# An encoder layer on one core: stores moved to ScalarE, v of the fourth kind sorted as it is stored, conditioning and combination spread over more token steps

## Chip, cores and metric

The kernel runs on one NeuronCore of a Trainium2 chip. The metric is the device time of one execution in microseconds (us), lower is better. Profiles show one execution each; the engines are called PE (TensorE, matmul), PEld (its weight loads), DVE (VectorE), ACT (ScalarE), POOL (GpSimd) and SP (SyncE).

## The reference

One layer of an encoder, float32, 1024 tokens of width 1024:

```python
mod = silu(c) @ w_ada + b_ada                      # conditioning: 6 rows of 1024
h = rms_norm(x, g_norm1) * (1 + sc1) + sh1
qa, ka, va, qb, kb, vb, gates = split(h @ w_in)
o_a = neighbourhood_attention(norm(qa), norm(ka), va, rpb)      # 8 heads, 16 x 64 grid
for g, (window, dilation) in enumerate(((128, 1), (512, 4), (2048, 16))):
    outs[g], lses[g] = dilated_window_attention(rot(norm(qb_g)), rot(norm(kb_g)), vb_g, window, dilation)
o_b = einsum(softmax(lses over g), outs)           # the three dilations combined
gate_a, gate_b = split(sigmoid(gates + b_gate))
x = x + gt1 * ((gate_a * (o_a @ w_proj_a) + gate_b * (o_b @ w_proj_b)) @ w_o)
h2 = rms_norm(x, g_norm2) * (1 + sc2) + sh2
a, up = split(h2 @ w_ffn_in)
x = x + gt2 * ((silu(a) * up) @ w_ffn_out)
```

## The kernel before

Every matrix product is made of three passes: each operand is rounded to a short part (whi, by ScalarE, L118) and the remainder (wlo, by POOL or VectorE, L119), and hi·hi, hi·lo and lo·hi are summed in PSUM.

The program has a start (normalisation, first conditioning rows), the **token steps** (about 60 to 615 us of the span), and an end (output projections and the feed-forward part). The change lies in the token steps, the loop `for n in range(6, 92)` with `u, t = divmod(n, 8)`:

- For u below 10, step n projects token tile t (128 tokens) to q, k and v of unit u: 8 chunks of three matmuls 128x384 (L305). A unit is a pair of heads. Kinds 0, 1 and 2 are the three dilations, two units each; **the fourth kind** (kind 3, units 6 to 9) is the neighbourhood attention. For the steps 80 to 91 the chunks are those of the gate product instead (`gate_pre`, L704), whose results are stored by SyncE (sig_d, L711).
- After the chunks, `proj_post` squares and copies q and k (ScalarE), sums (VectorE, L326), takes the reciprocal root (L129 to L134), and, for kinds 1 to 3, copies v to a tile vs (L343) and stores it to v_d in DRAM (L345). At the unit's last tile v is read back with its rows in the order that the kind's attention wants: for kind 3 by eight strided reads (L358).
- Between chunk 4 and chunk 5 stands the attention of earlier units. Before step 58 it works in clusters at odd steps; from step 58 on (`PAIRED`) in items at every step: scores (L468), softmax (L482 to L486), transposes (L494), their evacuation to PT (L498, L500), product with v (L509), evacuation to stg by VectorE (L512) and store by SyncE (L513). Clusters have L588 and L590 for the last two.
- `ada_step` adds one of 64 pieces of the conditioning: w_ada is loaded in pieces of 512 KB (wa, L288), one per two pieces, and VectorE adds it to acc (L292, L294). After eight pieces `ada_row` sums over partitions on PE (L271) and stores a row to mod_d (row, brow).
- `combine_prep` and `combine_step` combine the three dilations, in twelve parts: a part loads ut from DRAM (L643 to L650), VectorE spreads the factors to fb (L655), PE transposes fb (L664), and VectorE multiplies and adds (L672 to L675), at last storing to o_d (L677). Part ci = n − 64 is prepared at step n and taken at step n + 1.

The order on TensorE is that of the code (written out by hand). The orders on the other engines and on the queues come from a scheduler that models a timeline, with priorities (`urgent`), and each tile waits for a free buffer of its tag. One tag matters here: `raw`, six buffers of 128x512, holds the weights on their way to whi and wlo (`wload`), and also the combination's ut and fb and the conditioning's row and brow. The gate weights of step n and n + 1 are two such tiles, taken at even n by `gate_w` at the first chunk.

Of the kernel before, what the change touches and what calls it, by code (L numbers as in the profile page):

```python
# [12 lines left out]
AF = mybir.ActivationFunctionType  # L13
# [23 lines left out]
PAIRED, RBT, COMB = 58, 5, 64  # L37
# [6 lines left out]
def hybrid_layer(ctx: ExitStack, tc: tile.TileContext, x, colp, wada1, wada2, bada2, wqkv, wg, wpa, wpb,  # L44
                 wo, w1, w2, hgain, ropeg, rope, rbias, bmask, g2r, out):
    nc = tc.nc
# [104 lines left out]
    def big(name, shape=None, dtype=F32):  # L151
        return ap_.tile(shape or wide, dtype, tag="big", bufs=NBIG, name=name)
# [113 lines left out]
    ada_state = {"i": 0}  # L266
# [41 lines left out]
    def urgent(off):  # L308
        def deco(f):
            def g(*a):  # L310
                with tc.high_priority(off):
                    return f(*a)
            return g
        return deco

    @urgent(PP)
    def proj_post(U, t):
        pd = U.pd[t]
        qn = ap_.tile([128, 4, 64], F32, tag="qn", bufs=7, name="qn")
        U.qn[t] = qn  # L320
        pq = pd[:, :256].rearrange("p (h d) -> p h d", h=4)
        sq = ap_.tile([128, 256], F32, tag="sq", bufs=1, name="sq")
        nc.scalar.activation(sq, pd[:, :256], AF.Square)
        nc.scalar.activation(qn, pq, AF.Copy)
        ss = ap_.tile([128, 4], F32, tag="ss4", bufs=2, name="ss4")
        nc.vector.tensor_reduce(ss, sq.rearrange("p (h d) -> p h d", h=4), axis=mybir.AxisListType.X, op=ALU.add)  # L326
        r = rstd(ap_, 64, 4, ss, "q")
        nc.vector.tensor_tensor(qn, qn, r[:, :, None].to_broadcast([128, 4, 64]), op=ALU.mult)  # L328
        if U.kind < 3:
            ra = ap_.tile([128, 4, 16], F32, tag="ra", bufs=2, name="ra")  # L330
            rb = ap_.tile([128, 4, 16], F32, tag="rb", bufs=2, name="rb")
            tb = U.tab[:, t]
            v4 = lambda z: z.rearrange("p (a b) c -> p a b c", a=2)
            tv = lambda f, c0, c1: tb[:, f, :, None, c0:c1].to_broadcast([128, 2, 2, c1 - c0])
            nc.gpsimd.tensor_tensor(v4(ra), v4(qn[:, :, 0:16]), tv(0, 0, 16), op=ALU.mult)  # L335
            nc.gpsimd.tensor_tensor(v4(rb[:, :, 0:8]), v4(qn[:, :, 8:16]), tv(1, 0, 8), op=ALU.mult)
            nc.gpsimd.tensor_tensor(v4(rb[:, :, 8:16]), v4(qn[:, :, 0:8]), tv(1, 8, 16), op=ALU.mult)
            nc.gpsimd.tensor_tensor(qn[:, :, 0:16], ra, rb, op=ALU.add)
        if U.kind == 0:
            nc.scalar.activation(U.v[:, t, :], pd[:, 256:384], AF.Copy)  # L340
        else:
            vs = ap_.tile([128, 128], F32, tag="vs", bufs=2, name="vs")
            nc.scalar.activation(vs, pd[:, 256:384], AF.Copy)  # L343
            vd = v_d[U.u - 2]
            nc.sync.dma_start(vd[t * 128:(t + 1) * 128, :], vs)  # L345
            if t == 7:
                U.v = big("v", [128, 8, 128])
            if t == 7 and U.kind == 1:
                vv = vd.rearrange("(h i r) d -> h i r d", h=2, r=4)
                uv = U.v.rearrange("p (r h) d -> p h r d", h=2)  # L350
                for j in range(2):
                    nc.sync.dma_start(uv[:, j], vv[j])
            elif t == 7 and U.kind == 2:
                nc.sync.dma_start(U.v, vd.rearrange("(i u) d -> i u d", u=8))
            elif t == 7:
                vv = vd.rearrange("(r j c) d -> j c r d", r=16, c=8)
                for j in range(8):
                    nc.sync.dma_start(U.v[:, j, :], vv[j])  # L358

    @urgent(QT)  # L360
    def qk_turns(tiles, tag):
# [140 lines left out]
    @urgent(AV)  # L502
    def at_pv(I):
        U, nq, nkb = I.U, I.nq, I.nkb
        po = bank("v")
        for i in range(nkb):
            for h in range(2):
                hs = slice(h * 64, h * 64 + 64)
                nc.tensor.matmul(po[hs, :nq], U.v[:, I.kb0 + i, hs], I.PT[h][:, i, :nq],  # L509
                                 start=(i == 0), stop=(i == nkb - 1))  # L510
        st = ap_.tile([128, 128], F32, tag="stg", bufs=3, name="stg")
        nc.vector.tensor_copy(st[:, :nq], po[:, :nq])  # L512
        nc.sync.dma_start(I.dst, st[:, :nq])  # L513
        if I.last:
            unit_out(U)

# [54 lines left out]
    @urgent(AV)  # L571
    def cl_pv(C):
        po = bank("v")
        n, outs = 0, []
        for I in C.items:
            U, nq = I.U, I.nq
            for i in range(I.nkb):
                for h in range(2):
                    hs, c = slice(h * 64, h * 64 + 64), I.c0 + i * 128
                    nc.tensor.matmul(po[hs, n:n + nq], U.v[:, I.kb0 + i, hs], C.PT[h][:, c:c + nq],  # L580
                                     start=(i == 0), stop=(i == I.nkb - 1))
            if outs and outs[-1][0] is I.o:
                outs[-1][3] = n + nq
            else:
                outs.append([I.o, I.q0, n, n + nq])
            n += nq
        st = ap_.tile([128, 512], F32, tag="stg", bufs=3, name="stg")
        nc.vector.tensor_copy(st[:, :n], po[:, :n])  # L588
        for o, q0, a, b in outs:
            nc.sync.dma_start(o[:, q0:q0 + b - a], st[:, a:b])  # L590
        for I in C.items:
            if I.last:
                unit_out(I.U)
# [65 lines left out]
    def combine_step(i):  # L659
        pr, g, hf = i // 6, (i % 6) // 2, i % 2  # L660
        fb, ut, uv, acc = cb[i]
        pf = bank("t")
        for j in range(4):
            nc.tensor.transpose(pf[:, j * 128:(j + 1) * 128], fb[:, j].rearrange("p h d -> p (h d)"), ident)  # L664
        acc = acc[:, hf * 512:hf * 512 + 512]
        n = 1 if g == 0 else (4 if g == 1 else 8)

        def v(z):
            return z if g == 0 else z.rearrange("p (i r) -> p i r", r=n)

        if g == 0:
            nc.vector.tensor_mul(acc, ut, pf)  # L672
        else:
            nc.vector.tensor_mul(v(pf), uv, v(pf))
            nc.vector.tensor_add(acc, acc, pf)  # L675
        if g == 2 and hf == 1:
            nc.sync.dma_start(o_d[4 + pr], cb[i][3])  # L677
# [92 lines left out]
    U = new_unit(0, w0)  # L770
# [136 lines left out]
    for t in range(6):  # L907
        proj_post(U, t)
# [5 lines left out]
    for n in range(6, 92):  # L914
        u, t = divmod(n, 8)
        if u < 10:
            if t == 0:
                units.append(new_unit(u, [nextw[u, k] for k in range(KT)]))
            U = units[u]
# [16 lines left out]
                    ready.setdefault(8 * u + 2 + slot, []).append(I)  # L936
        if n == 8 * 7 + 5:
            combine_stats()
        ci = n - COMB
        if 0 <= ci < 12:  # L940
            combine_prep(ci)
        if n >= PAIRED:
            done, prev, cur = prev, cur, ready.pop(n, [])
# [46 lines left out]
        chunk()  # L990
        chunk()
        chunk()
        if n >= 8 and (t != 7 or u > 8) and ada_state["i"] < 65:
            ada_step()
        if 2 <= u < 6 and t < 5:
            if t in (2, 4):
# [4 lines left out]
                t_piece(2 * (u - 2) + t // 2, 1)  # L1001
        if n in (85, 88):
            w1_combos((n - 85) // 3, EARLY[(n - 85) // 3])
        if 1 <= ci < 13:
            combine_step(ci - 1)
        while chunks:
            chunk()
        if u < 10:
# [649 lines left out]
```

## Time and profile before

| | us |
|---|---|
| median of 3 runs | 1515.14 (1513.23 to 1521.24) |
| the profiled execution | 1508.57 |
| its span | 1506.8 |
| PE busy | 1486.2 (99%) |
| VectorE busy | 1098.1 (73%) |
| ScalarE busy | 656.3 (44%) |
| POOL busy | 537.1 (36%) |
| HBM traffic | 240 MB, 159 GB/s over the span |

A row of a group reads: line, engine, operation, output <- inputs, shape, count | busy time, mean ns of one | idle time of the engine just before them and what ended it. A row of the timeline reads: start, length, instruction, count, and in brackets the idle time before it and its releaser. SPq is SyncE's queue of DMA issues, ACTq is ScalarE's. PE is pipelined, so that its busy time is not its peak; its waits and its granted clock tell more.

### The profile page before, as it was taken

Reading aid. Unit: us, or ns where it says so; the run is one execution under the profiler, and the core shown is the slowest. Engines: PE = TensorE matmul, PEld = TensorE weight load, DVE = VectorE, ACT = ScalarE, POOL = GpSimd, SP = SyncE. Lnnn points to the kernel's source line nnn. Section 1 sums busy time; section 2 is a strip of 40 time slices with the busy share of each in tenths; the row PEclk is TensorE's granted clock in tenths of the full one; section 3 lists DMA queues with packets and bytes.
Section 4 is the critical chain, followed back from the end, with each engine's and each line's share of the span. In section 5 each row is a group of like instructions: output and inputs, shape, how many; then the busy total and the mean of one; then the engine's idle time right before and its main releaser. Section 6 shows DMA issues by size and latency. Waiting matters only on the chain. (4 is left out here: it accounts for less than half of the span.)

```text
span 1506.8 us, 24296 instructions
## 1 busy us (share of the span) xinstructions
PE 1486.2 (99%) x8156; PEld 1265.3 (84%) x8156; DVE 1098.1 (73%) x2318; ACT 656.3 (44%) x1638; POOL 537.1 (36%) x540
## 2 busy tenths in 40 slices
PE   9999999999999999999999999999999999999998
PEld 7999989998878877888888888888888888887886
DVE  6868777777889845466665597788767777599468
ACT  5655555555545543246432344233223323354442
POOL 0432333311100040002352301677767776104464
PEclk9999999999999999999999999999999999999999
DMA  9625444545145155834553225345433334798342
GB/s 371 226 85 186 141 153 143 192 137 166 59 126 169 62 179 154 318 98 126 168 188 137 92 90 186 119 131 182 155 127 108 109 105 147 268 380 280 98 150 102
DMA packets 154415, 241.66 MB, mean 160 GB/s; under 512 B 26657, under 2 KB 73377, under 8 KB 153521
## 3 DMA queue, kind: packets, MB, share of 16 engines
q1 hardware_dynamic: 153136, 235.90, 47.7%
q10 hardware_dynamic: 1152, 4.19, 0.7%
q8 instruction: 65, 1.06, 0.3%
q14 instruction: 62, 0.50, 0.1%
HBM read 179.89 MB, written 60.15 MB: 159 GB/s over the span
## 5 line engine op out<-in xcount | busy, mean ns | idle before, releaser
L119 POOL TENSOR_TENSOR wlo<-raw,whi 128x512 fp32r<-128x512 f32 (+2 forms) x133 | 172.5, 1310 | 463.4 <-ACT whi L118 435.3
L118 ACT ACTIVATE whi<-raw 128x512 fp32r<-128x512 f32 (+1 forms) x348 | 204.1, 599 | 260.0 <-PE ps_s L1493 35.4
L305 PE MATMUL ps_d<-whi,hT 128*128 128x384 f32 x1152 | 311.0, 341 | 0.0
L119 DVE TENSOR_TENSOR wlo<-raw,whi 128x512 fp32r<-128x512 f32 (+1 forms) x215 | 180.5, 852 | 75.2 <-ACT whi L118 70.8
L305 PEld LDWEIGHTS ps_d<-whi,hT 128*128 128x128 f32 x1152 | 210.3, 189 | 5.3 <-ACT vs L343 3.5
L305 PE MATMUL ps_d<-wlo,hT 128*128 128x384 f32 x576 | 193.6, 336 | 2.4 <-DVE wlo L119 2.0
L305 PEld LDWEIGHTS ps_d<-wlo,hT 128*128 128x128 f32 x576 | 108.9, 189 | 3.2 <-DVE wlo L119 2.3
L118 ACT ACTIVATE whi<-ws 128x512 fp32r<-128x512 f32 x65 | 40.8, 628 | 126.4 <-DVE ws L1340 74.2
L1273 POOL TENSOR_TENSOR e<-e,c 128x512 f32<-128x512 f32 x44 | 68.9, 1566 | 61.3 <-DVE c L1403 37.1
L335 POOL TENSOR_TENSOR ra<-qn,rtab 128x64 f32<-128x64 f32 x48 | 16.7, 348 | 153.4 <-DVE qn L328 138.4
L119 POOL TENSOR_TENSOR wlo<-m,whi 128x512 fp32r<-128x512 f32 x35 | 51.3, 1476 | 54.8 <-ACT whi L118 54.8
L1271 ACT ACTIVATE e<-e 128x512 f32<-128x512 f32 x44 | 27.5, 630 | 88.0 <-DVE e L1406 60.7
L547 ACT ACTIVATE P<-P,st 128x256 f32<-128x256 f32 (+2 forms) x100 | 45.5, 457 | 41.0 <-DVE st L545 41.0
L294 DVE SCALAR_TENSOR_TENSOR acc<-wa,cact,acc 128x512 f32<-128x512 f32 x56 | 43.2, 772 | 24.6 <-DMA wa<-in_wada_dram 24.6
L704 PE MATMUL ps_d<-hT,whi 128*128 128x512 f32 x192 | 60.6, 397 | 0.0
L483 ACT ACTIVATE P<-P,sx 128x384 f32<-128x384 f32 (+1 forms) x64 | 37.0, 580 | 51.4 <-DVE sx L482 51.4
L1323 PE MATMUL ps_v<-h2T,whi 128*128 128x512 f32 x192 | 59.2, 389 | 0.0
L1323 PE MATMUL ps_s<-h2T,whi 128*128 128x512 f32 x192 | 59.1, 389 | 0.0
L1323 PE MATMUL ps_d<-h2T,whi 128*128 128x512 f32 x184 | 56.7, 390 | 0.0
L129 ACT ACTIVATE ry<-ss,eps 128x4 f32<-128x4 f32 (+1 forms) x88 | 26.3, 299 | 69.5 <-DVE ss L326 67.2
L119 DVE TENSOR_TENSOR wlo<-ws,whi 128x512 fp32r<-128x512 f32 x45 | 50.3, 1117 | 8.2 <-ACT whi L118 8.1
L1272 DVE TENSOR_TENSOR e<-e 128x512 f32<-128x512 f32 x44 | 42.5, 974 | 17.3 <-ACT e L1271 17.2
(445 smaller groups left out, 3951.6 us busy)
## 6 DMA issues: line engine op xcount, KB each, us to landing
raw<-in_w_dram SPq DMA_DIRECT2D x139, 256.0 KB
ga_d<-e SPq DMA_DIRECT2D x77, 256.0 KB
raw<-ga_d SPq DMA_DIRECT2D x77, 256.0 KB
wa<-in_wada_dram SPq DMA_DIRECT2D x32, 512.0 KB
raw<-in_wqkv_dram SPq DMA_DIRECT2D x80, 192.0 KB
m<-in_w_dram SPq DMA_DIRECT2D x44, 256.0 KB
raw<-in_wg_dram SPq DMA_DIRECT2D x42, 256.0 KB
xt<-in_x_dram SPq DMA_DIRECT2D x16, 512.0 KB
```

Source lines behind the costliest of these rows:

```text
L118: nc.scalar.activation(hi[:, :n], r, AF.Copy)
L119: (eng or nc.gpsimd).tensor_sub(lo[:, :n], r, fview(hi[:, :n]))
L129: nc.scalar.activation(y, ss, AF.Ln, scale=1.0 / n, bias=eps)
L294: nc.vector.scalar_tensor_tensor(ada_acc[c], wa, cact[:, kk:kk + 1], ada_acc[c], op0=ALU.mult, op1=ALU.add)
L305: nc.tensor.matmul(pd[:, :384], tok(a, k, t), U.w[k][b][:, :384], start=(k == 0 and i == 0), stop=(k == KT - 1 and i == 2))
L483: nc.scalar.activation(P[:nq, :nk], P[:nq, :nk], AF.Exp, scale=-1.0, bias=nm, accum_out=sm)
L547: nc.scalar.activation(C.P[h][:nq, c], C.P[h][:nq, c], AF.Exp, scale=-1.0, bias=nm, accum_out=sm)
L704: nc.tensor.matmul(st["p"], gw[i, br][j][a][:, kk * 128:(kk + 1) * 128], hT[b][:, k, hs], start=(k == 0 and q == 0), stop=(k == 7 and q == 2))
L1271: nc.scalar.activation(sg, a, AF.Sigmoid)
L1272: nc.vector.tensor_mul(sg, sg, a)
L1273: nc.gpsimd.tensor_mul(sg, sg, up)
L1323: nc.tensor.matmul(pb, w[p][:, k * 128:(k + 1) * 128], b[q][:, k], start=(k == 0 and i == 0), stop=(k == 3 and i == 2))
```

## The change

1. The 64 stores of v (kinds 1 to 3) and the attention results' stores are issued by ScalarE instead of SyncE; the attention results are evacuated from PSUM by ScalarE instead of VectorE.
2. For kind 3 the store of v scatters the rows to the order that the attention wants, so that one plain read brings it back instead of eight strided ones.
3. From step 58 on, `ada_step` runs at even steps, and at every step after 76 (before: at nearly every step, until step 80; now until step 87).
4. The combination's part ci is prepared at step 64 + 2·ci and taken one step later (before: every step): it ends at step 87 instead of 76.

```diff
-            nc.sync.dma_start(vd[t * 128:(t + 1) * 128, :], vs)
+            if U.kind == 3:
+                nc.scalar.dma_start(vd.rearrange("(c r j) d -> r j c d", c=8, r=16)[2 * t:2 * t + 2], vs)
+            else:
+                nc.scalar.dma_start(vd[t * 128:(t + 1) * 128, :], vs)
...
-                vv = vd.rearrange("(r j c) d -> j c r d", r=16, c=8)
-                for j in range(8):
-                    nc.sync.dma_start(U.v[:, j, :], vv[j])
+                nc.sync.dma_start(U.v, vd.rearrange("(p j) d -> p j d", j=8))
...
-        nc.vector.tensor_copy(st[:, :nq], po[:, :nq])
-        nc.sync.dma_start(I.dst, st[:, :nq])
+        nc.scalar.activation(st[:, :nq], po[:, :nq], AF.Copy)
+        nc.scalar.dma_start(I.dst, st[:, :nq])
...
-        nc.vector.tensor_copy(st[:, :n], po[:, :n])
+        nc.scalar.activation(st[:, :n], po[:, :n], AF.Copy)
         for o, q0, a, b in outs:
-            nc.sync.dma_start(o[:, q0:q0 + b - a], st[:, a:b])
+            nc.scalar.dma_start(o[:, q0:q0 + b - a], st[:, a:b])
...
-        ci = n - COMB
-        if 0 <= ci < 12:
+        ci, odd = divmod(n - COMB, 2)
+        if 0 <= ci < 12 and not odd:
             combine_prep(ci)
...
-        if n >= 8 and (t != 7 or u > 8) and ada_state["i"] < 65:
+        if n >= 8 and (n % 2 == 0 or n > 76 if n >= PAIRED else t != 7) and ada_state["i"] < 65:
             ada_step()
...
-        if 1 <= ci < 13:
-            combine_step(ci - 1)
+        if 0 <= ci < 12 and odd:
+            combine_step(ci)
```

The lines after the change stand up to two higher by number (L345 becomes L346 and L348, L358 becomes L359, L513 becomes L514, L664 becomes L665, L704 becomes L705).

The order on TensorE changes only where the conditioning's sums and the combination's transposes go. Before, at the passage from step 79 (the last chunks of the projection) to step 80 (the gate product):

```order
L305 MATMUL ps_d<-whi,hT_406 128x384
L305 MATMUL ps_d<-whi,hT_112 128x384
L305 MATMUL ps_d<-wlo,hT_112 128x384
L305 MATMUL ps_d<-whi,hT_406 128x384
L704 MATMUL ps_d<-hT_112,whi 128x512
L704 MATMUL ps_d<-hT_406,whi 128x512
L704 MATMUL ps_d<-hT_112,wlo 128x512
```

Now a conditioning sum (acc to ps_t) and the transposes of fb, which end step 79, stand directly ahead of the first gate matmul:

```order
L305 MATMUL ps_d<-whi,hT_112 128x384
L305 MATMUL ps_d<-wlo,hT_112 128x384
L305 MATMUL ps_d<-whi,hT_406 128x384
L271 MATMUL ps_t<-acc_6327,ones 1x512
L665 MATMUL ps_t<-ident,fb 128x128 x4
L705 MATMUL ps_d<-hT_112,whi 128x512
L705 MATMUL ps_d<-hT_406,whi 128x512
L705 MATMUL ps_d<-hT_112,wlo 128x512
```

What moved are those two rows, which stood in earlier steps before; the gate matmuls themselves are the same.

On SyncE, the loads of the gate weights (raw<-in_wg) of step 80 stood before the change among the stores of the projection's v (v_d) and the attention's results (o_d), several steps ahead, with a conditioning weight (wa) before them:

```order
L288 DMA wa_7665<-in_wada_dram 128x1024
L111 DMA raw<-in_wg_dram 128x512
L345 DMA v_d<-vs 128x128
L111 DMA raw<-in_wg_dram 128x512
L274 DMA brow<-in_bada_dram 1x512
L513 DMA o_d<-stg 128x128
L345 DMA v_d<-vs 128x128
L513 DMA o_d<-stg 128x128
L345 DMA v_d<-vs 128x128
L677 DMA o_d<-oacc 128x1024
L513 DMA o_d<-stg 128x128
```

Now the first of them stands behind the combination's load for step 80 (ut), and the second behind the row of the conditioning (mod_d) and the read-back of v:

```order
L288 DMA wa_7669<-in_wada_dram 128x1024
L647 DMA ut<-u_d 128x4x128
L111 DMA raw<-in_wg_dram 128x512
L276 DMA mod_d<-row 1x512
L359 DMA v<-v_d 128x1024
L111 DMA raw<-in_wg_dram 128x512
L647 DMA ut<-u_d 128x4x128
L111 DMA raw<-in_wg_dram 128x512 x2
L651 DMA ut<-u_d 128x8x64
```

What moved: the two loads stand behind transfers of step 79 and 80 instead of some steps ahead of the last stores of v, and v is read once. In the order after the change, the first load's buffer is the one that held fb of the transposes quoted above, and it waits for them.

For the gate weights of step 88, SyncE before had them far ahead, between the stores of the gate results (sig_d) of steps 80 and 81:

```order
L711 DMA sig_d<-gsig 128x512
L111 DMA raw<-in_wg_dram 128x512
L276 DMA mod_d<-row 1x512
L111 DMA raw<-in_wg_dram 128x512 x5
L513 DMA o_d<-stg 128x128
L111 DMA raw<-in_wg_dram 128x512 x4
L711 DMA sig_d<-gsig 128x512
L111 DMA raw<-in_wg_dram 128x512 x3
```

Now they follow the stores of step 86's and step 87's gate results, ahead of the conditioning's last row:

```order
L712 DMA sig_d<-gsig 128x512
L765 DMA w_d<-w1m 128x512 x2
L712 DMA sig_d<-gsig 128x512 x2
L111 DMA raw<-in_wg_dram 128x512
L276 DMA mod_d<-row 1x512
L111 DMA raw<-in_wg_dram 128x512 x2
L678 DMA o_d<-oacc 128x1024
L111 DMA raw<-in_wg_dram 128x512 x12
```

What moved: the first load of step 88 has gone behind both stores of step 87's time, as its buffer is taken after row and brow of the conditioning's last sum, which step 87 makes; w1m and w_d are combinations of the feed-forward part's weights and stand ahead of it.

## The prediction

> **What bounds the kernel now.** I read the page's table of engines first, then the table by stage, then PE's waits, then what stood in front of each. The page's row gives busy time, share of the span and instructions:
>
> ```profile
> PE 1486.2 (99%) x8156; PEld 1265.3 (84%) x8156; DVE 1098.1 (73%) x2318; ACT 656.3 (44%) x1638; POOL 537.1 (36%) x540
> ```
>
> TensorE is the bound, and the change leaves its instructions and nearly their order as they are. So the change can win only what TensorE waits, and only in the stretch that it touches, the token steps (about 60 to 615 us). Stages of that stretch (length, then busy time of PE, PEld, DVE, ACT, POOL, then the granted clock, the DMA share and GB/s):
>
> ```profile
> 364.00:400.00 36.00, 33.74 (x214) 29.24 (x215) 26.58 (x95) 18.05 (x61) 0.40 (x1) 0.95 0.31 108
> 400.00:440.00 40.00, 36.35 (x272) 31.70 (x270) 34.52 (x112) 19.50 (x67) 5.04 (x5) 1.00 0.47 145
> 480.00:530.00 50.00, 47.80 (x347) 41.57 (x346) 43.75 (x144) 24.19 (x82) 2.99 (x2) 1.00 0.30 97
> 530.00:580.00 50.00, 50.00 (x295) 38.55 (x295) 25.39 (x74) 22.97 (x58) 18.49 (x14) 1.00 0.65 197
> ```
>
> VectorE is the fuller of the helpers where the conditioning, the combination and the fourth kind's attention meet (34.5 of 40 us), ScalarE has room (19.5), and the gate steps from 530 us on have no gap at all. PE's waits over 60 to 615 us (total, times, longest):
>
> ```profile
> PE ps_t L494 <- DVE oacc L672: 2.3, 1, 2.3
> PE ps_t L494 <- DVE P L486: 2.1, 2, 1.2
> PE ps_d L305 <- DVE wlo L119: 2.0, 1, 2.0
> PE ps_t L664 <- ACT PT L500: 1.4, 2, 1.1
> PE ps_t L494 <- DVE oacc L675: 1.2, 1, 1.2
> PE ps_v L369 <- POOL qn L338: 0.5, 1, 0.5
> PE ps_v L369 <- DVE qn L328: 0.5, 2, 0.3
> PE ps_d L305 <- POOL wlo L119: 0.4, 1, 0.4
> PE ps_t L494 <- DVE rv L130: 0.4, 1, 0.4
> PE ps_t L664 <- DVE PT L498: 0.3, 1, 0.3
> ```
>
> They add up to 11.1 us. The largest, on TensorE's and then on VectorE's timeline (start, length, instruction, idle time before it and its releaser):
>
> ```profile
> 371.97 0.44 PE L494 MATMUL ps_t<-ident,P 128*128 128x128 f32 x2 [1.24 <-DVE P L486]
> 373.23 0.46 PE L494 MATMUL ps_t<-ident,P 128*128 128x128 f32 x2 [0.82 <-DVE P L486]
> ...
> 425.88 0.44 PE L494 MATMUL ps_t<-ident,P 128*128 128x128 f32 x2 [2.33 <-DVE oacc L672]
> ...
> 429.48 0.66 PE L664 MATMUL ps_t<-ident,fb 128*128 128x128 f32 x4 [1.05 <-ACT PT L500]
> ```
>
> ```profile
> 423.69 1.54 DVE L294 SCALAR_TENSOR_TENSOR acc<-wa,cact,acc 128x512 f32<-128x512 f32 x2 [3.98 <-DMA wa<-in_wada_dram]
> 425.14 0.68 DVE L672 TENSOR_TENSOR oacc<-ut,ps_t 128x512 f32<-128x512 f32 x1
> ```
>
> VectorE stood 3.98 us at a conditioning weight (L294) that had not landed; L672, queued behind it, frees the PSUM bank that L494 needs. The weight was late because of SyncE's queue:
>
> ```profile
> 412.69 4.90 SPq L358 DMA_DIRECT2D v<-v_d  x8
> 417.70 0.40 SPq L345 DMA_DIRECT2D v_d<-vs  x1
> 418.20 0.38 SPq L513 DMA_DIRECT2D o_d<-stg  x1
> 418.62 0.42 SPq L288 DMA_DIRECT2D wa<-in_wada_dram  x1
> ```
>
> Eight issues of the read-back of v take 4.90 us, two stores follow, and only then goes the load; it is used 5.1 us after its issue (423.69 − 418.62).
>
> The pair at 371.97 and 373.23 also cost clock: the row 364:400 has a granted clock of 0.95, so 36 × 0.05 = 1.8 us. The lone 2.33 us at 425.88 left its row at 1.00. All that can be won is therefore 11.1 + 1.8 = 12.9 us, 0.85% of the time.
>
> **The change part by part.**
>
> *Stores to ScalarE, evacuations from VectorE to ScalarE, one read of v instead of eight, conditioning and combination at every other step.* The groups of 364 to 530 us (busy, mean ns; idle before) and ScalarE's own issue of a DMA:
>
> ```profile
> L294 DVE SCALAR_TENSOR_TENSOR acc<-wa,cact,acc 128x512 f32<-128x512 f32 x20 | 15.6, 781 | 8.6 <-DMA wa<-in_wada_dram 8.6
> L674 DVE TENSOR_TENSOR ps_t<-ut,ps_t 128x512 f32<-128x512 f32 x8 | 8.5, 1064 | 0.7 <-PE ps_t L664 0.7
> L129 ACT ACTIVATE ry<-ss,eps 128x4 f32<-128x4 f32 x22 | 6.5, 297 | 28.9 <-DVE ss L326 28.7
> L512 DVE COPY stg<-ps_v 128x128 f32<-128x128 f32 x21 | 6.0, 284 | 0.0
> L818 ACTq DMA_DIRECT2D h_d<-yT x8: 326/326/337, 28.7 to 53.8; - x8
> ```
>
> VectorE loses one 0.28 us copy per step here, half of L294 and half of the combination; SyncE loses 7 × 0.6 = 4.3 us of issues per unit of the fourth kind and both stores of each step. So the conditioning loads go out earlier and are asked for later. I count the L672 wait as gone (2.3), the two L486 waits as gone with their clock (2.1 + 1.8), L675 as 0.4 left (0.8 won), L664 and L119 as halved (0.9 and 1.0), the rest as staying but for 0.3: 9.2 us won. From below: if only the read-back matters, 4; from above, all 12.9.
>
> ScalarE pays per step two issues of 0.33 us and a copy that took VectorE 0.28 us, about 1 us of a step of some 6. The store of v stands ahead of L129, which waits anyway: 28.7 us over 22 steps, 1.3 us per step, for VectorE's sum (L326). So two thirds of it are hidden. If that cover is gone, L129 and all behind it come up to 0.7 us later in a step, and 30 such steps would give at most some 20 us, but only if TensorE waited on each, and L129's results are used two steps on. A store on ScalarE can also stand at its queue for an earlier transfer, with the exponential L483 and the evacuation L500 behind it; before, such waits stood on SyncE and no row shows them on ScalarE. Bounds 0 (the waits are past by then) to 4 us (four waits of the 1.05 us of row 429.48, which is PE waiting for ScalarE); I take 1, one such wait. Nothing below zero, as a store earlier on ScalarE frees nothing that TensorE waits for beyond what is counted.
>
> *The gate weights of step 80.* Here the change adds a wait. The weights' buffers are shared with the combination's tiles (ut, fb) and the conditioning's (row, brow). Before, the combination was over at step 76, and the loads for step 80 went out long ahead (SyncE, then TensorE's first use):
>
> ```profile
> 489.34 0.43 SPq L111 DMA_DIRECT2D raw<-in_wg_dram  x1
> ...
> 491.12 0.33 SPq L111 DMA_DIRECT2D raw<-in_wg_dram  x1
> ```
>
> ```profile
> 524.62 0.63 PE L704 MATMUL ps_d<-hT,whi 128*128 128x512 f32 x2
> ```
>
> 35 us of lead. Now all six buffers are held at step 79 by the combination of steps 76 and 78 and by row/brow, and the first gate load waits for the combination's transposes at the end of step 79, the very instruction in front of the first gate matmul. TensorE then stands for the load, the rounding on ScalarE, and the remainder on POOL. Their prices: load to use on SyncE and ScalarE, and POOL's group.
>
> ```profile
> 534.03 0.38 SPq L111 DMA_DIRECT2D raw<-in_wg_dram  x1
> ...
> 546.20 2.84 SPq L111 DMA_DIRECT2D raw<-in_wg_dram  x3
> ```
>
> ```profile
> 539.06 1.25 ACT L118 ACTIVATE whi<-raw 128x512 fp32r<-128x512 f32 x2 [5.47 <-DMA raw<-in_wg_dram]
> ...
> 544.71 0.68 ACT L710 ACTIVATE gsig<-ps_d,cp 128x512 f32<-128x512 f32 x1
> ...
> 549.18 0.63 ACT L118 ACTIVATE whi<-raw 128x512 fp32r<-128x512 f32 x1 [1.60 <-DMA raw<-in_wg_dram]
> ```
>
> ```profile
> L119 POOL TENSOR_TENSOR wlo<-raw,whi 128x512 fp32r<-128x512 f32 x14 | 18.5, 1345 | 58.9 <-ACT whi L118 58.8
> ```
>
> From issue to first use: 539.06 − 534.03 = 5.0 us with other loads beside it, and 549.18 − 546.20 = 3.0 for the first of three. I take the middle, 4.0, as neither fits better. Then 0.63 of L118, then 1.35 of POOL less the 0.5 us in which TensorE does the two matmuls that need only whi: 4.0 + 0.63 + 0.85 = 5.5 us (4.5 to 6.5).
>
> *The gate weights of step 88.* Same buffers, another queue: the load now stands on SyncE behind the store of step 87's gate result (sig_d), which needs L710 after TensorE's last matmul of step 87. So 0.1 + 0.68 (L710) + 0.36 (a store's issue) = 1.1 us later, less what TensorE still has to do, four transposes (0.66, row 429.48) and one conditioning sum:
>
> ```profile
> L271 PE MATMUL ps_t<-acc,ones 128*1 128x512 f32 x2 | 1.0, 590 | 0.0
> ```
>
> 1.1 + 5.5 − 0.66 − 0.59 = 5.3 us (4.3 to 6.3). The gate steps had no wait to hide it in (50.00 of 50.00). Steps 82, 84, 86 and 90 keep a lead of two steps or more: nothing.
>
> *The clock after those two gaps.* Waits of 2.1 us in all, close together, cost 1.8 us in the row 364:400; a single 2.33 cost none. Gaps of 5.4 are nearer to the first: 1.8 each, 3.6 (0 to 3.6). The Trainium skill, "TensorE: Matmul & The Clock Gate", Part 1: The HAM clock gate, says that the array goes to half clock after a free-running window of about 3.4 us spent idle and needs such a window of work to come back. By it 1.7 us per drop, and a 5.4 us gap holds a whole window in some 6 cases of 10, an estimate of 2.0 us for both instead of 3.6, so a sum lower by 1.6. This trace does not agree with the idle window as told: waits of 1.24 and 0.82 us were enough.
>
> **Sum.** −9.2 + 1.0 + 5.5 + 5.3 + 3.6 = +6.2 us. On the profiled execution's 1508.57 us (span 1506.8) that is 1514.8; that execution lies 6.6 us under the median of the runs, 1515.14, and on the median it is 1521.3, so 1521.
>
> **The rivals.**
>
> *The two stalls and the old waits together (slower).* If the conditioning loads are late because the transfers themselves are slow, and not because of SyncE's queue, VectorE still stands in front of the combination's evacuations. For it: 5.1 us from issue to use at 418.62, with the queue's part over by then. Against it: half of the asks. Then L672, L486 and their clock (6.2 us) stay: +12.4, 1527.5. It decides if more than 1.3 us of those 6.2 remain, as 0.5% is 7.5 us. The Trainium skill, "DMA: Bandwidth & Descriptors", Issuing engines are not separate DMA queues, speaks for it: spreading issues over engines saves only the issuing, since all share the same DMA engines. The issue alone was 4.90 us here, which the trace shows to be no small thing.
>
> *The stalls do not come (faster).* If the loads land in under 3 us and the gate matmuls find their weights with a wait of 1 us or less, the sum is −9.2 + 1 + 2 = −6.2, and −10 with everything won: 1505 to 1509. For it: no such wait stands in the trace of before. Against it: no row of a gate load is shorter than 3.0 us.
>
> *ScalarE becomes what TensorE waits for (slower).* In the combination's steps ScalarE goes from 19.5 of 40 us to about 27, and its stores may stand before L483. 4 us instead of 1 gives +9.2, 1524. Against it: its present waits are mostly on VectorE, which gets lighter.
>
> *It doesn't do what it says.* With the loads no earlier in time and the gaps half as long, gains (4) and losses (6) cancel: +2, 1517.
>
> **How the numbers follow.** My forecast (+2 to +10, 1517 to 1525) has 0.50, of which 0.13 lies beyond 0.5%; late transfers 0.22; ScalarE 0.05; no stalls 0.13, of which 0.08 beyond 0.5%; cancelling 0.10. 0.5%, 7.5 us, is about what a measurement of this kernel can tell from no change. So slower 0.13 + 0.22 + 0.05 = 0.40, faster 0.08, same 0.52. Range: low end −9.2 of gain (the middle) with both stalls at their least and no clock loss, −9.2 + 4.5 + 4.3 = −0.4, widened to −5 for part of the rival without stalls, 1510; high end gain 4, stalls 6.5 + 6.3, clock 3.6, ScalarE 4 = +16.4, 1531.
>
> **What would show it.** Right: in the table by stage, PE loses about 5 us once around 525 us and once around 590 us, with the first gate matmul waiting on whi or wlo and the granted clock below 1 there; L672 and L486 gone from PE's waits; L294's idle time on the load below 8.6 us. Wrong in its main step: gate matmuls that start without a wait, or a gate load issued well ahead of step 79's end. Wrong in the gain: L494 still waiting for L672 or L486.

## The result, and the profile after

The change made the kernel slower: 1524.34 us (median of 6 runs, 1521.78 to 1526.16) against 1516.0 (6 runs, 1511.02 to 1521.24), ratio 1.0064 with a 95% interval of 1.0046 to 1.0081. The forecast was 1521 in a range of 1510 to 1531; the time lies in the range and on the side of the forecast's sum. By the prediction's own line of 0.5% it is "slower", to which 0.40 was given, and not "same", which had 0.52.

The profiled execution has a span of 1522.9 us. Its row of engines, and the stages of the token steps with those of them cut where the gate steps 80 and 88 begin (length, busy time of PE, PEld, DVE, ACT, POOL, then the granted clock, DMA share, GB/s):

```profile
PE 1491.8 (98%) x8156; PEld 1269.1 (83%) x8156; DVE 1083.5 (71%) x2265; ACT 669.7 (44%) x1691; POOL 535.7 (35%) x540
```

```profile
364.00:400.00 36.00, 33.37 (x220) 30.27 (x219) 26.76 (x93) 18.34 (x66) 0.00 (x0) 0.95 0.24 83
400.00:440.00 40.00, 40.00 (x293) 35.01 (x292) 32.79 (x117) 23.95 (x84) 5.30 (x5) 1.00 0.42 130
520.00:540.00 20.00, 16.44 (x93) 12.53 (x94) 7.71 (x31) 7.67 (x21) 5.12 (x4) 0.83 0.48 135
...
580.00:615.00 35.00, 29.88 (x165) 22.23 (x164) 14.73 (x35) 14.39 (x33) 9.98 (x8) 0.90 0.56 171
```

Before, the steps from 530 us on had no gap (50.00 of 50.00); now 20 us around 530 lose 3.6, 35 us before 615 lose 5.1. The stage of the wait for L672 (400 to 440) is full now, and the one before it (364 to 400) is as it was, its clock of 0.95 too. PE's waits (60 to 640 us; the rows of before's table to compare are L672 and the two for L486):

```profile
PE ps_d L705 <- ACT whi L118: 9.9, 2, 5.0
PE ps_s L469 <- DVE qk L395: 2.6, 1, 2.6
PE ps_t L495 <- DVE P L487: 2.2, 1, 2.2
PE ps_d L305 <- DVE wlo L119: 2.0, 1, 2.0
PE ps_v L370 <- POOL qn L338: 1.3, 2, 1.0
PE ps_t L495 <- DVE oacc L676: 0.9, 2, 0.5
PE ps_d L305 <- ACT vs L343: 0.6, 1, 0.6
PE ps_d L305 <- POOL wlo L119: 0.4, 1, 0.4
```

They add up to 19.9 us, 8.8 more than before. The two of 5.0 us are the first gate matmuls of steps 80 and 88. In place, with the load's issue on SyncE and its rounding on ScalarE:

```profile
368.96 0.51 PE L469 MATMUL ps_s<-qk 64*128 64x256 f32 x4 [2.63 <-DVE qk L395]
...
523.43 1.22 PE L705 MATMUL ps_d<-hT,whi 128*128 128x512 f32 x2 [4.96 <-ACT whi L118]
...
595.56 1.22 PE L705 MATMUL ps_d<-hT,whi 128*128 128x512 f32 x2 [4.98 <-ACT whi L118]
...
619.33 0.44 PE L495 MATMUL ps_t<-ident,P 128*128 128x128 f32 x2 [2.18 <-DVE P L487]
```

```profile
518.50 0.33 SPq L111 DMA_DIRECT2D raw<-in_wg_dram  x1
...
582.00 8.11 SPq L712 DMA_DIRECT2D sig_d<-gsig  x2
590.20 0.38 SPq L111 DMA_DIRECT2D raw<-in_wg_dram  x1
...
592.89 15.51 SPq L111 DMA_DIRECT2D raw<-in_wg_dram  x12
608.44 0.91 SPq L759 DMA_DIRECT2D w1m<-in_w_dram  x2
```

```profile
522.75 0.63 ACT L118 ACTIVATE whi<-raw 128x512 fp32r<-128x512 f32 x1 [3.81 <-DMA raw<-in_wg_dram]
...
594.88 1.27 ACT L118 ACTIVATE whi<-raw 128x512 fp32r<-128x512 f32 x2 [5.11 <-DMA raw<-in_wg_dram]
```

The load of step 80 goes out at 518.50, as step 79's transposes end, and that of step 88 at 590.20, behind the stores of sig_d: 4.25 and 4.68 us to first use, as the prediction priced them (3.0 to 5.0).

The third wait, at 619.33, is a follow-up that was not foreseen. The late load of step 88 holds up the twelve loads behind it, so the loads for the feed-forward part's combinations (w1m) go out at 608.44; in the profile before they went out at 592.75. VectorE takes its instructions in order and stands at them, with the softmax's L487 behind:

```profile
366.25 1.54 DVE L294 SCALAR_TENSOR_TENSOR acc<-wa,cact,acc 128x512 f32<-128x512 f32 x2 [4.06 <-DMA wa<-in_wada_dram]
...
368.30 0.61 DVE L395 TENSOR_TENSOR qk<-ps_v,qk 128x256 fp32r<-128x256 f32 x1
...
617.59 0.69 DVE L760 TENSOR_TENSOR w1m<-w1m 128x512 f32<-128x512 f32 x1 [2.94 <-DMA w1m<-in_w_dram]
```

The upper rows are the same figure at 366 us: the conditioning's weight is late there as before (4.06 us), and only the instruction behind it is another one, L395 in place of L486. But it is no longer SyncE's queue that makes it late. Its load and its use in the kernel before, where the load stands behind eight reads of v, and then its load now, behind one read:

```profile
363.70 0.41 SPq L288 DMA_DIRECT2D wa<-in_wada_dram  x1
...
367.73 0.75 DVE L294 SCALAR_TENSOR_TENSOR acc<-wa,cact,acc 128x512 f32<-128x512 f32 x1 [4.07 <-DMA wa<-in_wada_dram]
```

```profile
359.30 0.89 SPq L288 DMA_DIRECT2D wa<-in_wada_dram  x2
```

The load goes out 4.4 us earlier, but the weight is used only 1.5 us earlier: from issue to use it was 4.0 us before and is 6.9 now, and in those 6.9 us the DMA engines are 0.90 busy. The time that the queue gave back went into the transfer.

Behind each of the waits at 523, 595 and 619 us the clock is at half, or a little above, for some 4 us. Behind step 80's wait in the change:

```profile
523.40:525.40 2.00, 1.84 (x4) 1.02 (x5) 0.00 (x0) 0.63 (x1) 1.27 (x1) 0.50 0.72 236
525.40:527.40 2.00, 2.00 (x6) 1.61 (x5) 0.00 (x0) 0.00 (x0) 1.28 (x1) 0.50 0.44 129
527.40:529.40 2.00, 2.00 (x13) 1.20 (x14) 0.00 (x0) 0.63 (x1) 0.72 (x1) 0.95 0.47 133
```

4.0 us at 0.50 is 2.0 us lost. The same reading behind step 88 gives 1.9 (2 us at 0.50 and 2 at 0.55) and behind 619 us 1.7 (2 at 0.64, 2 at 0.51).

So the two profiles add up. From 60 to 640 us: waits +8.8, clock +2.0 +1.9 +1.7, and a wait of 0.9 on a load (L724) at 651 us: +15.3 (the last is not shown to be the change's, as the same load costs 0.7 in the second profile of before), where the spans differ by 1522.9 − 1506.8 = 16.1. That is twice what the medians differ by (8.3). The first profile of before was one of its shorter executions; why, the second one shows, below.

### The profile page after: what moved, and what is told of

Same layout as the page of the kernel before. It is cut to its first block, busy times and chain, and to the rows that moved or that the text cites. A ratio compares the mean times of both kernels' runs of the same rounds, so it can differ in the third digit from the quotient of the medians.

```text
span 1522.9 us, 24174 instructions
## 1 busy us (share of the span) xinstructions
PE 1491.8 (98%) x8156; PEld 1269.1 (83%) x8156; DVE 1083.5 (71%) x2265; ACT 669.7 (44%) x1691; POOL 535.7 (35%) x540
## 4 chain that ended last, share of the span: by engine, by line
PE 78%; DMA 9%; DVE 7%; ACT 3%; issue 2%; POOL 1%; SPq 1%; ACTq 0%; DVEq 0%; POOLq 0%
PE ps_d L305 13%; PE ps_v L1324 7%; PE ps_d L1324 7%; PE ps_s L1324 7%; PE ps_t L1324 6%; PE ps_d L705 4%; PE ps_s L1494 3%; PE ps_d L1494 3%; PE ps_d L1259 2%; PE ps_s L1259 2%; PE ps_v L1494 2%; PE ps_t L1494 2%; DVE wlo L119 2%; DMA wa<-in_wada_dram 2%; PE ps_v L1259 1%
## 5 line engine op out<-in xcount | busy, mean ns | idle before, releaser
L705 PE MATMUL ps_d<-hT,whi 128*128 128x512 f32 x192 | 64.8, 420 | 9.9 <-ACT whi L118 9.9
L294 DVE SCALAR_TENSOR_TENSOR acc<-wa,cact,acc 128x512 f32<-128x512 f32 x56 | 42.1, 751 | 24.6 <-DMA wa<-in_wada_dram 24.4
L483 DVE CUSTOM_DVE_ANT_0 P<-ps_s,rb 128x384 f32<-128x384 f32 (+1 forms) x64 | 31.9, 520 | 29.1 <-PE ps_s L469 29.0
```

Source lines behind the costliest of these rows:

```text
L294: nc.vector.scalar_tensor_tensor(ada_acc[c], wa, cact[:, kk:kk + 1], ada_acc[c], op0=ALU.mult, op1=ALU.add)
L483: nc.vector.tensor_tensor_reduce(P[:nq, :nk], pS[:nq, :nk], I.masks[h], -1.0, 3.0e38, ALU.add, ALU.min, nm)
L705: nc.tensor.matmul(st["p"], gw[i, br][j][a][:, kk * 128:(kk + 1) * 128], hT[b][:, k, hs], start=(k == 0 and q == 0), stop=(k == 7 and q == 2))
```

## The experiments

Each kernel was run beside the kernel before; the ratios are to that, with 95% intervals. An edit is to the changed kernel where no other one is named. Line numbers are those of the kernel at hand.

### Without the third and fourth part

```diff
-        ci, odd = divmod(n - COMB, 2)
-        if 0 <= ci < 12 and not odd:
+        ci = n - COMB
+        if 0 <= ci < 12:
...
-        if n >= 8 and (n % 2 == 0 or n > 76 if n >= PAIRED else t != 7) and ada_state["i"] < 65:
+        if n >= 8 and (t != 7 or u > 8) and ada_state["i"] < 65:
...
-        if 0 <= ci < 12 and odd:
-            combine_step(ci)
+        if 1 <= ci < 13:
+            combine_step(ci - 1)
```

> The change without its third and fourth part (conditioning and combination at the steps of before; stores and evacuations on ScalarE, v of the fourth kind sorted in the store). Theory (the loss is all from the spread, which makes the gate weights of steps 80 and 88 late; the rest gains): no wait at the first gate matmuls, about 8 us under before, 1508. Rival (ScalarE's stores cost): at or over before, 1516 to 1520, with PE waiting for ScalarE. Rival (the gain of 10 us up to step 79 came from the spread): within 3 us of before.

1509.19 us, 0.9972 (0.9955 to 0.9988). No wait at the gate matmuls. So the loss comes from the spread, and the stores with the sorted v are a gain, of half the size that was expected. What is left in PE's waits of it, at the top:

```profile
PE ps_t L665 <- DVE PT L499: 4.3, 2, 2.4
```

The combination still waits, for an evacuation on VectorE (L499) in place of its own. In front of it VectorE stands 2.2 us for a conditioning weight (L294, 418 us), as in the kernel before.

### Only the third and fourth part

The edit is the reverse of the one above, in the kernel before.

> The kernel before with only the third and fourth part (conditioning and combination spread; stores on SyncE as before). Theory: two waits of about 5 us at steps 80 and 88 with the clock lost behind them and the third one at step 91, 20 us in all, less 2 to 5 us for a lighter VectorE: 1531 to 1534. Rival (the spread is harmless, ScalarE's stores cost): within 3 us of before, 1513 to 1519, and no long wait at the first gate matmuls.

1520.88 us, 1.0045 (1.0029 to 1.0061): slower, through the same waits, but by less than expected.

```profile
PE ps_d L704 <- ACT whi L118: 8.3, 2, 4.2
...
PE ps_t L494 <- DVE P L486: 1.4, 2, 0.8
```

The third wait is not there, and L672 has gone: the spread alone, without any store moved, takes the wait for L672 away.

### The gate weights' buffers taken early

```diff
+        if n in (77, 85):
+            gate_w((n - 77) // 4, 0)
         ci, odd = divmod(n - COMB, 2)
```

> The whole change, but the gate weights of steps 80 and 88 take their buffers at steps 77 and 85, ahead of the combination's and the conditioning's tiles. Theory (shared buffers make those loads late): both waits gone, the one at step 91 too, 17 to 21 us under the change, 1503 to 1508, the fastest of all. Rival (the loads are late for another reason, SyncE's queue or the transposes themselves): waits of 5 us stay, 1520 to 1526. Rival (ScalarE's stores cost): waits gone but no faster than before, 1514 to 1518.

1505.88 us, 0.9950 (0.9929 to 0.9970), the lowest median of all: 18 us under the change by two lines that add no work. Both gate waits are gone, and the one at step 91 with them. What is left at the top of PE's waits, beside the 2.2 us at 213 us that every profile so far has in much the same length:

```profile
PE ps_s L469 <- DVE qk L395: 2.4, 1, 2.4
PE ps_t L724 <- DMA tg<-t_d: 1.1, 1, 1.1
```

### The kernel before, once more

> The kernel before once more, unchanged, for a second profile of it. If the waits of the first profile are the same each time, PE waits about 11 us in the token steps with the same two at 372 and 426 us, and the span is 1507. If the medians of before (1516) hold waits that the first profile (1508.57) did not have, they show here as longer or other waits, with a span of 1510 to 1519.

A span of 1513.7 us. PE's waits are nearly those of the first profile (12.3 us in the token steps against 11.1):

```profile
PE ps_t L494 <- DVE oacc L672: 2.8, 1, 2.8
PE ps_t L494 <- DVE P L486: 2.0, 2, 1.2
PE ps_d L305 <- DVE wlo L119: 2.0, 1, 2.0
```

What differs is the clock behind them. The wait of 2.02 us at 213 us stands in both profiles at the same length. The 2 us from 215 on, in the first profile of before and in this one:

```profile
215.00:217.00 2.00, 2.00 (x20) 1.74 (x18) 1.71 (x9) 1.29 (x6) 0.49 (x3) 1.00 0.35 105
```

```profile
215.00:217.00 2.00, 2.00 (x9) 1.56 (x7) 1.67 (x10) 1.05 (x5) 0.74 (x3) 0.50 0.14 40
...
364.00:400.00 36.00, 32.50 (x206) 28.83 (x205) 24.31 (x90) 16.26 (x58) 0.00 (x0) 0.91 0.33 112
400.00:440.00 40.00, 36.97 (x256) 31.95 (x256) 33.40 (x107) 19.71 (x65) 5.45 (x5) 0.96 0.45 139
```

At the same wait the clock stayed at 1.00 in one execution and went to 0.50 in the other; at 425 us the first lost none and this one 40 × 0.04 = 1.6. With 36 × 0.09 = 3.2 and 25 × 0.07 = 1.7 at 213 (0.93 from 205 to 230 us) that makes 6.5 us of clock against 1.8, and with 1.2 more of waits 5.9 of the 6.9 by which the spans differ. So a wait of 2 us costs 2 us or 3.7, and its length does not decide which: of the 13 profiles of this document that have this wait (1.85 to 2.20 us), five lost clock behind it (0.93 from 205 to 230 us) and eight did not (1.00), and each outcome stands beside a wait of 2.02 and beside one of 2.20 us. One profile of a kernel with many such waits is not its median.

### The conditioning spread, the combination as before

```diff
-        ci, odd = divmod(n - COMB, 2)
-        if 0 <= ci < 12 and not odd:
+        ci = n - COMB
+        if 0 <= ci < 12:
...
-        if 0 <= ci < 12 and odd:
-            combine_step(ci)
+        if 1 <= ci < 13:
+            combine_step(ci - 1)
```

> The whole change but for its fourth part: the combination at every step from 64 to 76 as before, the conditioning spread. Theory (it is the combination's ut and fb that hold the gate weights' buffers): no wait at the first gate matmuls of steps 80 and 88. The gain up to step 79 lies between that of no spread (5 us) and of all of it (8 us), so 1506 to 1510 where before is 1514. Rival (the conditioning's late last row, at step 87, is enough to make the load of step 88 late): one wait of 4 to 5 us there, 1514 to 1518.

1521.35 us, 1.0053 (1.0036 to 1.0071): the theory fell. The rival held on the wait at step 88, but not on the time, which is 3 us above its range. With the combination over at step 76, the load of step 88 is as late as ever (PE, then SyncE):

```profile
592.94 1.22 PE L705 MATMUL ps_d<-hT,whi 128*128 128x512 f32 x2 [4.65 <-ACT whi L118]
```

```profile
588.09 0.32 SPq L712 DMA_DIRECT2D sig_d<-gsig  x1
588.50 0.38 SPq L111 DMA_DIRECT2D raw<-in_wg_dram  x1
```

So for step 88 it is the conditioning's last row, which step 87 now makes, and not the combination. It is also not a lack of buffers: the six loads before it were rounded, and their remainders made, by 537 us. The load goes out as VectorE begins the row (L275, 588.39). It waited for its turn behind the row; how the scheduler's order comes to that with buffers empty, no run here shows.

At step 80 the waits are smaller here, 1.63 us for whi and 0.72 for wlo, and of another kind. Both loads went out 20 us ahead, and ScalarE's rounding, which waits for no load, stands behind the last work of step 79 (SyncE, then ScalarE):

```profile
502.80 2.73 SPq L111 DMA_DIRECT2D raw<-in_wg_dram  x2
```

```profile
522.41 1.14 ACT L118 ACTIVATE whi<-raw 128x512 fp32r<-128x512 f32 x2
```

So the conditioning alone does not make the load of step 80 late.

### The spread and the early buffers alone

The edits of the second and the third experiment, in the kernel before: stores on SyncE, evacuations on VectorE, eight reads of v.

> The kernel before with the spread (third and fourth part) and the gate weights' buffers taken early, but with all stores on SyncE, the evacuations on VectorE and eight reads of v. Theory now (the gain up to step 79 comes from the spread, by asking VectorE for less at a time, and not from the stores): 5 to 9 us under before, 1505 to 1509 where before is 1514, and within 3 us of the whole change with early buffers. Rival (the prediction's cause: SyncE's queue relieved of stores and of seven reads brings the loads in time): within 3 us of before, with L672 or L486 still in PE's waits.

1508.24 us, 0.9959 (0.9944 to 0.9975). The theory holds, at the lower edge of its gain: freed of the late loads, the spread is a gain by itself. L672 is gone from PE's waits; L486 is still there with 1.2 us in two waits, as the rival had it.

### Conditioning weights loaded one step earlier

```diff
         if kk % 2 == 0:
-            ada_acc["w"] = big("wa2", [128, 2, 512])
-            nc.sync.dma_start(ada_acc["w"], wada2[c, :, kk:kk + 2, :])
+            ada_acc["w"] = ada_acc.pop(("n", i)) if i else ada_load(i)
...
+        if kk % 2 == 1 and i < 63:
+            ada_acc["n", i + 1] = ada_load(i + 1)
```

(in the kernel with early buffers; `ada_load` holds the two lines removed)

> The whole change with early gate buffers, and each conditioning weight loaded one step of the conditioning earlier. Theory (VectorE stands in order at a late weight, and PE's waits of 2.2 us at 213 and 2.4 us at 369 are behind it): both gone, 3 to 6 us under the whole change with early buffers, 1500 to 1503 where before is 1514. Rival (the loads go out no earlier, as buffers and SyncE's order decide): 1504 to 1507.

1510.82 us, 0.9981 (0.9967 to 0.9995): higher than without it (0.9950, the intervals just overlap), and not the gain of either forecast. Of the two waits one went (at 213 us, 0.4 left) and one stayed (2.6 for qk), and others came, in steps that had none (2.1 more for vs, L350):

```profile
PE ps_s L476 <- DVE qk L402: 2.6, 1, 2.6
PE ps_v L377 <- POOL qn L345: 2.5, 2, 1.7
```

Neither theory had that. Whether the earlier loads took the place of others was not followed up here.

### Only the sorted store of v

```diff
-            nc.sync.dma_start(vd[t * 128:(t + 1) * 128, :], vs)
+            if U.kind == 3:
+                nc.sync.dma_start(vd.rearrange("(c r j) d -> r j c d", c=8, r=16)[2 * t:2 * t + 2], vs)
+            else:
+                nc.sync.dma_start(vd[t * 128:(t + 1) * 128, :], vs)
...
-                vv = vd.rearrange("(r j c) d -> j c r d", r=16, c=8)
-                for j in range(8):
-                    nc.sync.dma_start(U.v[:, j, :], vv[j])
+                nc.sync.dma_start(U.v, vd.rearrange("(p j) d -> p j d", j=8))
```

(in the kernel before)

> The kernel before with only the second part: v of the fourth kind sorted as it is stored (by SyncE) and read back by one transfer. Theory now (the queue's part is the smaller one): 0 to 3 us under before, 1511 to 1514 where before is 1514, with the wait of VectorE at the conditioning weight shorter than 3.98 us but L672 or L486 still in PE's waits. Rival (the prediction's floor: the read-back alone brings 4 us): 1508 to 1510. Third way (a scattered store costs): above before.

1509.42 us, 0.9974 (0.9959 to 0.9989), about 4 us: more than I then thought, and what the prediction gave as its floor for the read-back. The two waits for L486 at 372 us are gone, and with them the clock's loss:

```profile
350.00:400.00 50.00, 48.84 (x335) 43.44 (x333) 41.27 (x138) 27.30 (x89) 5.26 (x5) 1.00 0.36 119
```

L672 is gone too, but not its cause. VectorE still stands at the conditioning weight, 2.59 us in place of 3.98 (the load follows the one read of v and takes 5.5 us from issue to use, 5.1 before), and TensorE waits longer than before, for an evacuation on ScalarE that waits in its turn for VectorE, and loses 1.6 us of clock behind it (0.96 over 400 to 440 us). VectorE's row, then TensorE's:

```profile
415.35 0.75 DVE L294 SCALAR_TENSOR_TENSOR acc<-wa,cact,acc 128x512 f32<-128x512 f32 x1 [2.59 <-DMA wa<-in_wada_dram]
```

```profile
419.38 1.11 PE L665 MATMUL ps_t<-ident,fb 128*128 128x128 f32 x4 [3.36 <-ACT PT L501]
```

The gain is also that of the run without the spread (0.9972), which has the whole first part, stores and evacuations on ScalarE, beside it. So of the first part these two runs show nothing, neither gain nor loss.

### The combination spread, the conditioning as before

```diff
-        if n >= 8 and (n % 2 == 0 or n > 76 if n >= PAIRED else t != 7) and ada_state["i"] < 65:
+        if n >= 8 and (t != 7 or u > 8) and ada_state["i"] < 65:
```

> The whole change but for its third part: the conditioning at the steps of before (its last row at step 80), the combination spread to step 87. Theory now (the conditioning's last rows at steps 79 and 87 take their place among the buffers just ahead of the gate weights, which have to follow them; the combination's tiles alone do no harm): no long wait at the first gate matmuls of steps 80 and 88, 5 to 9 us under before, 1504 to 1508 where before is 1512.5. Rival (the prediction's cause for step 80, the combination's ut and fb hold the buffers): the wait of 5 us at step 80 stays, 1511 to 1516.

1514.96 us, 1.0015 (0.9999 to 1.0032). On the gate weights the theory holds: no wait at the first gate matmuls of steps 80 and 88, though the combination runs to step 87: the loads of step 80 go out at 502.37 and 504.24, 13 us ahead. On the time it missed by 7 us; the time lies in the rival's range, but for another reason. Late waits take their place, VectorE's rows first and PE's behind them:

```profile
566.97 0.69 DVE L760 TENSOR_TENSOR w1m<-w1m 128x512 f32<-128x512 f32 x1 [3.57 <-DMA w1m<-in_w_dram]
...
572.71 0.69 DVE L676 TENSOR_TENSOR oacc<-oacc,ps_t 128x512 f32<-128x512 f32 x1
```

```profile
573.54 0.52 PE L495 MATMUL ps_t<-ident,P 128*128 128x128 f32 x3 [2.81 <-DVE oacc L676]
```

It is the picture of 425 us in the kernel before: VectorE stands at a late load, then works without a gap, the combination's L676 stands in that row, and L495 lacks the bank. The combination was moved into steps in which another late load, w1m, takes the place of wa.

### The second to fourth part with early buffers

The sorted store above, in the kernel with the spread and the early buffers alone; the stores stay on SyncE, the evacuations on VectorE.

> The second, third and fourth part with early gate buffers, the first part left out: stores on SyncE, evacuations on VectorE. Theory (the sorted store and the spread are the gains, ScalarE's stores little): 6 to 9 us under before, 1503.5 to 1506.5 where before is 1512.5, as good as the whole change with early buffers (0.995). Rival (the stores on ScalarE bring their own 2 to 3 us): as the spread with early buffers alone, 1507 to 1510.

1506.99 us, 0.9961 (0.9947 to 0.9975), 0.5 us above the theory's range and at the edge of the rival's. The intervals of this, of the one without the sorted store (0.9959) and of the whole change with early buffers (0.9950) overlap. So the sorted store adds nothing that can be told to the spread, though alone it is worth 0.26%. That fits two edits which act on the same waits: each takes L672 away, and L486 is gone with the one and down to 1.2 us with the other.

### The change, once more

> The whole change once more for a second profile and times beside before on this chip. Theory: the same waits of 5.0 us at steps 80 and 88 and of 2 us at step 91, each with clock lost behind it, 1521 to 1526, 8 to 10 us over before. If the clock behind a wait is a matter of chance, the stages' granted clocks differ from the first profile's while the waits are the same.

1524.76 us, 1.0078 (1.0056 to 1.0100), span 1522.1. Waits of 4.2 and 4.5 us at the gate matmuls, with 1.1 more for wlo behind them; at step 91 only 0.8 in place of 2.2. The clocks differ, 0.91 from 520 to 540 us in place of 0.83, but as the waits differ too this run does not decide whether that is chance. Against the second profile of before the span is 8.4 us longer, the difference of the medians.

### Three pieces of the conditioning moved away from 360 us

```diff
-        if n >= 8 and (n % 2 == 0 or n > 76 if n >= PAIRED else t != 7) and ada_state["i"] < 65:
+        if n >= 8 and n not in (56, 57, 58) and (n % 2 == 0 or n > 70 if n >= PAIRED else t != 7) and ada_state["i"] < 65:
```

(in the kernel with early buffers)

> The whole change with early gate buffers, and the conditioning's pieces of steps 56, 57 and 58 moved to steps 71, 73 and 75. Theory (VectorE takes its instructions in order and stands 3.6 to 4.1 us at a late conditioning weight at 361 to 366 us; TensorE's wait of 2.4 us at 369 for VectorE's L395 is behind it): that wait gone with the clock lost behind it, 2 to 4 us under the whole change with early buffers, 1501 to 1504 where before is 1513, ratio 0.992 to 0.994. Rival (the wait moves to where the pieces now are, or L395 is late for another reason): ratio 0.994 to 0.997.

1509.66 us, 0.9971 (0.9955 to 0.9987): no gain, the rival held. The wait did not go:

```profile
365.04 1.54 DVE L294 SCALAR_TENSOR_TENSOR acc<-wa,cact,acc 128x512 f32<-128x512 f32 x2 [4.11 <-DMA wa<-in_wada_dram]
```

Fewer pieces stand there, but the first still comes as late. Its load had gone out in good time:

```profile
358.15 0.42 SPq L288 DMA_DIRECT2D wa<-in_wada_dram  x1
```

It takes 6.9 us from issue to use, with the DMA engines 0.95 busy at 294 GB/s. Beside it stand the one read of v (512 KB, issued 0.4 us ahead) and the two loads of rb (384 KB each, right behind). With the weight's own 512 KB that is 1.8 MB, an estimate of 6 us at this rate. So the load is late through the transfers beside it; no run moved those, so this stays a reading of the trace.

## Why the prediction was right, and where it was not

**The two gate waits: right.** 5.5 and 5.3 us were forecast, 4.96 and 4.98 came; the early buffers took both away. The clock behind them: 1.8 each was forecast, 2.0 and 1.9 came. The estimate of 2.0 for both together, worked out from the Trainium skill, "TensorE: Matmul & The Clock Gate", Part 1: The HAM clock gate, was too low. That the window runs freely, as the Trainium skill says there, agrees with the two profiles of before: behind the same wait of 2.02 us the clock was 1.00 once and 0.50 once. That a whole window of about 3.4 us has to be idle does not agree: 2.02 us were enough.

**The cause at step 80 and 88: right for step 80, half right for step 88.** For step 80 the prediction had all six buffers held by the combination and row/brow together. The runs with one half of the spread agree: with either half as before, the loads go out 13 or 20 us ahead, and only with both spread does the first one go out as late as the end of step 79 (518.50; 518.67 in the run with only the third and fourth part). With the conditioning alone spread there is a wait of 1.63 us, but for ScalarE's rounding and not for a load. For step 88 the prediction named the same buffers, and the store of sig_d ahead of the load. Here the conditioning's last row at step 87 is enough by itself: without the combination the wait stays (4.65), without that row it is gone. In the run with the conditioning alone spread the buffers were empty, so it was the turn that the load waited for, not the room.

**The gain: the step that failed in size.** 9.2 us were counted, of them L672 and L486 with their clock as gone. PE's waits up to 520 us fell from 11.1 to 7.8, by 3.3. What failed is the step that took the L486 waits and their clock as gone because the loads go out earlier. L672 went, as was said. In place of L486 came the 2.6 us for L395, behind the same late weight (4.06 us; 4.07 at this place in the profile before), and the stage kept its clock of 0.95. That is the first rival's mechanism, weighed at 0.22, at this one place: the queue let the load out 4.4 us earlier, and the transfer took 2.9 us longer (6.9 for 4.0). The reason given for the gain was wrong in part, too. The relief of SyncE by ScalarE's stores cannot be told from nothing (0.9972 with them and 0.9974 without; with the spread and early buffers 0.9950 and 0.9961, intervals that overlap). That agrees with the Trainium skill, "DMA: Bandwidth & Descriptors", Issuing engines are not separate DMA queues, by which several issuing engines save only the time of the issue. The sorted store with its seven reads saved does show (0.9974), and so does the spread of conditioning and combination (0.9959 with early buffers).

**What was left out.** The wait at step 91, 2.2 us and 1.7 of clock: the prediction followed the late load of step 88 to TensorE and not to what is queued behind it on SyncE, twelve gate loads and then w1m. That is 3.9 us; the 0.9 on L724 was not in the sum either.

**ScalarE: 1 us forecast**, 0.6 came (vs, L343, 334 us).

**The sum.** On its own base, the first profile, the forecast of +6.2 stands against +15.3: the gain less ScalarE's cost was 3.3 in place of 8.2, the gate waits 9.9 in place of 10.8, their clock 3.9 in place of 3.6, and 4.8 were missing (step 91 and L724). That it came within 3 us of the median owes something to that profile, which had lost 1.8 us of clock where the second one lost 6.5: the median of before has more of the old waits' cost in it, and the change loses less against it. The clocks on record fit that: 0.999 over the first profile's execution, a mean of 0.9956 over the 20 executions of before beside the first experiments, only one of them at 0.999. The sign and the range were earned by the gate waits; the nearness of the figure was not.

## What to carry to other kernels

When work is spread over later steps, look at what shares its buffers: tiles of one tag are taken in the order of the program, and here a row of 2 KB taken at step 87 cost the weights of step 88 their lead, with buffers empty (before, by their order on the queue, their loads went out from 541 us on for a use at 587). It cost two lines to take the buffers ahead of it, and that turned a loss of 0.6% into a gain of 0.5%. Follow a late load to the end of its queue: the wait at step 91 stood three steps behind its cause. And when a queue is relieved, count the bytes beside the load as well as the issues ahead of it: here a load that went out 4.4 us earlier was of use 1.5 us earlier.

## What the runs showed of the hardware that was not expected

Whether the clock drops behind a wait of about 2 us is not settled by the wait: behind the same one at 213 us (1.85 to 2.20 us) it fell in five of 13 profiles, to 0.72 over the 6 us from 213 us on, and stayed at 1.00 in eight. Two profiles of one kernel differed by 6.9 us (1506.8 and 1513.7) with waits that differ by 1.2 in all.

From issue to use, a conditioning weight of 512 KB took 4.0 us behind eight issues of 64 KB reads that had gone out over 5.0 us, and 6.9 us right behind one read of the same 512 KB, with two loads of 384 KB right after it: the queue was relieved, the transfers were not.
